# One woven sequence for the gate/up and down parts of each SwiGLU, in an order written out by hand, and weight splits in halves

## The chip, the cores and the metric

The kernel runs on one core of a Trainium2 chip. The metric is the device time of one execution in microseconds (us). A core has five engines that run side by side: TensorE (PE in the profile, with its weight loads as PEld), VectorE (DVE), ScalarE (ACT), GpSimd (POOL) and SyncE (SP), whose queue here issues the transfers. Each engine takes its instructions in the order in which the program lists them for it. SBUF is the on-chip memory; PSUM holds the results of matmuls in banks of 128x512 f32.

## What is computed

One layer over 1024 tokens of width 1024, all in f32. The change touches the two SwiGLUs (`D_FF` = 2816), and slightly the mixers and the cross-attention in between:

```python
def swiglu(h, w_gu, w_down):
    gu = h @ w_gu
    gate, up = jnp.split(gu, 2, axis=-1)
    return (jax.nn.silu(gate) * up) @ w_down

def reference(x, mem, ...):
    ...
        x = x + 0.5 * swiglu(rmsnorm(x, ffn1_norm[l]), ffn1_w_gu[l], ffn1_w_down[l])
        h = rmsnorm(x, mix_norm[l])
        proj = h @ w_in[l]
        ...
        x = x + mixed @ w_out[l]
        x = x + memory_cross_attention(rmsnorm(x, mem_q_norm[l]), rmsnorm(mem, mem_kv_norm[l]),
                                       mem_w_q[l], mem_w_kv[l], mem_w_o[l])
        x = x + 0.5 * swiglu(rmsnorm(x, ffn2_norm[l]), ffn2_w_gu[l], ffn2_w_down[l])
    return rmsnorm(x, final_norm)
```

## The kernel before

**Numbers in two parts.** Every f32 operand of a matmul is split into a rounded half `hi` (a Copy on ACT) and the remainder `lo` (a subtraction on DVE). A product is then three matmuls: hi by hi, hi by lo, lo by hi (`mm3`, L113 to L117).

**Layout.** x is held transposed in sixteen tiles `xT[c, hf]` of 128x512: `c` counts 128 columns of the model, `hf` the two halves of the tokens. `rs[hf]` holds 1/rms of each token, spread over the partitions; the lifted tiles `hT` (names hh and hl) hold x times the gain of the norm, and `rs` is multiplied in after the matmul.

**Seven products for eight.** `swiglu` (L547) cuts each pair of column blocks into a 2x2 of blocks and multiplies them by Strassen's scheme in Winograd's form. `PRODUCTS` (L212) lists the seven products of one job: the factor of the weights (A11, A12, A22 or a sum S1 to S4, made on POOL at L235 to L244), the factor of the activations (B11, B21, B22 or a sum T1 to T4), and the bank X, Y or Z into which the product is accumulated. A bank is read between products, since X passes from A11 to S2 to S3 to A22. A product of four blocks is twelve matmuls (L258 to L260).

**Jobs and weaving.** A `job` (L216) is the seven products of one pair of weight blocks: `factor` loads the weights on SP (L335), makes the sum on POOL, hi on ACT (L342) and lo on DVE (L343). `weave` (L263) takes two streams of jobs, the second three products behind the first (`LAG`), and alternates their products; `prepare` makes factors up to six products ahead (`AHEAD`). After each product `read` takes the bank: for gate/up an ACT copy (L615) or a DVE add (L622), then SiLU and two multiplications by `rs` (L632, L598, L599, L643); for down a DVE `scalar_tensor_tensor` into `xT` (L754).

**The order of a SwiGLU.** Eleven pairs of gate and up blocks come first. Pair 0 is multiplied plainly (gate before the call, up at L593 to L698). `sums` (L556) makes T1 to T4 from x, x is stored to DRAM and its tiles are given up (L677, L678) for tiles E of the gate/up results. Then `pairs.run()` (L708) weaves ten gate jobs with ten up jobs; each pair's result and its four sums are stored to DRAM (`store`, L683). Only after it comes a second weave (L763): down in groups of 4, 4 and 3 pairs (4, 4 and 2 in SwiGLU 2, with the last pair done plainly at its end), the pieces read back by `staged` (L715) through four buffers sg, the tiles of x by `fetch` (L725). In SwiGLU 1 the chunks of x that are finished are squared for the next norm and lifted for the mixers (`arrive`, L157; `lift_chunk`, L168). `normalise_memory` (L488) prepares the memory input beside pair 5 and later.

**What sets the order.** The program names operations in the order of the Python text, but the scheduler beneath places each engine's instructions by its own model of time and by when their operands are ready. An operation can so be put ahead of one that was written earlier. `tc.issue_after` fixes that one comes behind another on the same engine.

**Mixers and attention** load weights by columns (`load_cols`, L99, 128x8x128) or rows (`load_rows`, L108) and split them by `split` (L91): one ACT copy (L95) and one DVE subtraction (L96) of 1024 elements a partition.

Of the kernel before, what the change touches and what calls it, by code (L numbers as in the profile page):

```python
# [18 lines left out]
P = 128  # L19
# [12 lines left out]
def hybrid_layer(ctx, tc, x, mem, ffn1_norm, ffn1_w_gu, ffn1_w_down, mix_norm, w_in, hg_lb_raw,  # L32
# [37 lines left out]


# [19 lines left out]
    def split(pl, tag, src, shape=None, eng=None, bufs=None, ends="hl"):  # L91

        shape = shape or [P, src.shape[-1]]
        hi, lo = (pl.tile(shape, F32R, name=tag + end, bufs=bufs) for end in ends)
        nc.scalar.activation(hi, src, AF.Copy)  # L95
        (eng or nc.vector).tensor_tensor(lo, src, hi.bitcast(F32), op=ALU.subtract)  # L96
        return hi, lo
# [42 lines left out]
    def rsqrt(ss, n, scale, keep=""):  # L140
# [5 lines left out]
        nc.vector.tensor_scalar(ms, ss, scale, EPS, op0=ALU.mult, op1=ALU.add)  # L146
        nc.vector.tensor_scalar(b, ms.bitcast(I32), 1, None, op0=ALU.logical_shift_right)
        nc.vector.tensor_scalar(y.bitcast(I32), b, -1.0, RSQRT_SEED, op0=ALU.mult, op1=ALU.add)
        for _ in range(3):
            nc.vector.tensor_tensor(u, y, y, op=ALU.mult)  # L150
            nc.vector.scalar_tensor_tensor(u, u, -0.5, ms, op0=ALU.mult, op1=ALU.mult)
            nc.vector.scalar_tensor_tensor(y, u, 1.5, y, op0=ALU.add, op1=ALU.mult)
# [4 lines left out]
    def arrive(c, hf, g0, sqp, acc, lift=True, eng=None):  # L157

        sq = (accp if hf else sqp).tile([P, H], F32, name="sqa") if hf not in acc else sqp.tile([P, H], F32, name="sq", bufs=2)
        nc.scalar.activation(sq, xT[c, hf], AF.Square)  # L160
        if hf in acc:
            nc.gpsimd.tensor_tensor(acc[hf], acc[hf], sq, op=ALU.add)
        else:
            acc[hf] = sq
        if lift:
            lift_chunk(c, hf, g0, eng)

    def lift_chunk(c, hf, g0, eng=None):  # L168
        g = G[:, g0 + c:g0 + c + 1]
        hi = hp.tile([P, H], F32R, name=f"hh{c}_{hf}")  # L170
        lo = hp.tile([P, H], F32R, name=f"hl{c}_{hf}")
        nc.scalar.activation(hi, xT[c, hf], AF.Copy, scale=g)
        (eng or nc.vector).scalar_tensor_tensor(lo, xT[c, hf], g, hi.bitcast(F32), op0=ALU.mult, op1=ALU.subtract)
        hT[hf][c] = (hi, lo)

    def inv_rms(hf, acc, psn, tag):

        ps = psn.tile([P, H], F32, name=tag)
        for t in range(4):
            nc.tensor.matmul(ps[:, t:t + 1], acc[hf][:, t * P:(t + 1) * P], ones, start=True, stop=True)  # L180
        return rsqrt(ps[:, 0:4], 4, 1.0 / D, f"h{hf}")

    def inv_rms_both(acc, psn, tag):
        ps = psn.tile([P, H], F32, name=tag)
        for hf in range(2):
            for t in range(4):
# [1302 lines left out]
```

## Time and profile before

| | |
|---|---|
| time, median of 3 runs | 2348.41 us (2341.6, 2348.91, 2348.41) |
| the profiled execution | 2342.71 us |
| its span, first to last instruction | 2340.7 us |
| mean granted clock of TensorE in it | 0.987 |
| moved by DMA | 226.98 MB, mean 97 GB/s |

The profiled execution is one run; its span is 2.0 us less than its time. In the profile a row of the timeline gives the start, the duration, the engine, the line of the kernel, the operation, its output and inputs with their shapes, and in brackets how long the engine was idle before it and what it waited for. A group's row ends in the busy time and the mean of one in ns, then the idle time before and its causes. A waits row gives the total, how many times, and the longest. SwiGLU 1 fills the span from about 41 to 692 us, the mixers and the attention the time to about 1670, SwiGLU 2 the rest.

### The profile page before, as it was taken

To read this page: it belongs to the slowest core of one execution; us is meant where nothing else is said; L and a number is where in the kernel's file an instruction comes from. 1 tells how busy PE (TensorE), PEld (TensorE's weight loads), DVE (VectorE), ACT (ScalarE), POOL (GpSimd) and SP (SyncE) were. 2 spreads that over 40 slices of the span, in tenths; PEclk is the share of its full clock that TensorE was granted. 3 is DMA by queue.
4 is the path that set the end of the run, shared out by engine and by line. 5 is a ranking of instruction groups with operands and counts; after the bars stand their busy time and mean duration, and the time that the engine had idled before them with its cause. 6 is when DMAs were issued, how large, how long until landed. Compare 5 with 4: busy or idle time off the path is not lost.

```text
span 2340.7 us, 31188 instructions
## 1 busy us (share of the span) xinstructions
PE 2232.2 (95%) x11314; PEld 1869.8 (80%) x11314; DVE 1602.7 (68%) x2768; ACT 980.3 (42%) x1791; POOL 765.0 (33%) x720
## 2 busy tenths in 40 slices
PE   8899999889999999999999999999979999989998
PEld 6788878777878788887978888887768888877787
DVE  6755665768774878878697546567755555586777
ACT  6433443435454635345364333234533333343444
POOL 3555555522240202011022020001356565642223
PEclk9999999999999999999999999999989999999999
DMA  6232343465331000000014411111333333255432
GB/s 221 89 110 95 130 135 110 144 215 178 120 121 38 28 28 28 28 28 28 19 46 147 124 37 54 46 37 46 124 99 110 114 103 117 91 175 191 143 104 81
DMA packets 197529, 226.98 MB, mean 97 GB/s; under 512 B 10688, under 2 KB 139776, under 8 KB 197376
## 3 DMA queue, kind: packets, MB, share of 16 engines
q1 hardware_dynamic: 197376, 225.00, 29.7%
q8 instruction: 89, 1.46, 0.3%
q14 instruction: 64, 0.52, 0.1%
HBM read 165.45 MB, written 59.51 MB: 96 GB/s over the span
## 4 chain that ended last, share of the span: by engine, by line
PE 75%; DVE 12%; ACT 4%; issue 4%; POOL 3%; DMA 2%; SPq 0%; ACTq 0%; DVEq 0%; POOLq 0%
PE X L258 8%; PE X L259 8%; PE X L260 8%; PE acc L115 4%; PE acc L117 4%; PE acc L116 4%; PE Y L258 4%; PE Y L259 4%; PE Y L260 4%; DVE om L925 2%; PE Z L260 2%; PE Z L259 2%; PE Z L258 2%; PE q L115 2%; PE q L116 2%
## 5 line engine op out<-in xcount | busy, mean ns | idle before, releaser
L343 DVE TENSOR_TENSOR f<-S,f 128x512 fp32r<-128x512 f32 (+2 forms) x256 | 211.9, 830 | 175.6 <-ACT f L342 162.5
L342 ACT ACTIVATE f<-S 128x512 fp32r<-128x512 f32 (+2 forms) x256 | 155.1, 608 | 217.4 <-PE X L260 90.7
L258 PE MATMUL X<-T,f 128*128 128x512 f32 x488 | 196.3, 402 | 38.9 <-ACT E L615 15.4
L343 DVE TENSOR_TENSOR f<-r,f 128x512 fp32r<-128x512 f32 (+2 forms) x208 | 172.7, 833 | 65.8 <-ACT f L342 65.6
L258 PE MATMUL X<-hh,f 128*128 128x512 f32 x488 | 191.4, 392 | 14.2 <-DVE x L754 6.6
L259 PE MATMUL X<-T,f 128*128 128x512 f32 x488 | 195.0, 399 | 0.0
L260 PE MATMUL X<-T,f 128*128 128x512 f32 x488 | 194.8, 399 | 0.0
L342 ACT ACTIVATE f<-r 128x512 fp32r<-128x512 f32 (+2 forms) x208 | 125.6, 610 | 159.1 <-PE X L260 90.1
L259 PE MATMUL X<-hl,f 128*128 128x512 f32 x488 | 190.1, 389 | 0.0
L260 PE MATMUL X<-hh,f 128*128 128x512 f32 x488 | 190.0, 389 | 0.0
L235 POOL TENSOR_TENSOR S<-r,r 128x512 f32<-128x512 f32 (+2 forms) x64 | 95.2, 1488 | 188.3 <-DMA r<-in_ffn_w_down_dram 117.5
L115 PE MATMUL acc<-hh,wh 128*128 128x512 f32 (+1 forms) x384 | 152.8, 398 | 0.0
L117 PE MATMUL acc<-hh,wl 128*128 128x512 f32 (+1 forms) x384 | 145.2, 378 | 0.0
L116 PE MATMUL acc<-hl,wh 128*128 128x512 f32 (+1 forms) x384 | 144.6, 377 | 0.0
L258 PEld LDWEIGHTS X<-T,f 128*128 128x128 f32 x488 | 94.9, 195 | 61.7 <-ACT E L615 16.3
L922 POOL TENSOR_SCALAR_AFFINE_SELECT om<-om 128x128 f32<-128x128 f32 x64 | 25.4, 397 | 354.0 <-ACT om L917 353.8
L241 POOL TENSOR_TENSOR S<-r,S 128x512 f32<-128x512 f32 (+2 forms) x64 | 81.6, 1275 | 165.2 <-DVE f L343 162.2
L244 POOL TENSOR_TENSOR S<-r 128x512 f32<-128x512 f32 (+2 forms) x64 | 97.3, 1520 | 107.9 <-DVE f L343 99.3
L599 POOL TENSOR_TENSOR E<-E,rs 128x512 f32<-128x512 f32 x84 | 121.1, 1443 | 31.0 <-ACT E L598 25.8
L598 ACT ACTIVATE E<-E 128x512 f32<-128x512 f32 x84 | 52.9, 631 | 186.0 <-POOL E L632 165.8
L632 POOL TENSOR_TENSOR E<-E,rs 128x512 f32<-128x512 f32 x60 | 100.6, 1677 | 89.6 <-DVE E L622 89.6
L258 PEld LDWEIGHTS X<-hh,f 128*128 128x128 f32 x488 | 91.7, 188 | 37.2 <-ACT f L342 8.2
(451 smaller groups left out, 6449.9 us busy)
## 6 DMA issues: line engine op xcount, KB each, us to landing
r<-in_ffn_w_gu_dram SPq DMA_DIRECT2D x86, 512.0 KB
r<-in_ffn_w_down_dram SPq DMA_DIRECT2D x34, 512.0 KB
wraw<-in_w_in_dram SPq DMA_DIRECT2D x20, 512.0 KB
wraw<-in_mem_w_kv_dram SPq DMA_DIRECT2D x16, 512.0 KB
T<-in_x_dram SPq DMA_DIRECT2D x8, 512.0 KB
fx<-x SPq DMA_DIRECT2D x16, 256.0 KB
x<-fx SPq DMA_DIRECT2D x16, 256.0 KB
xs<-x SPq DMA_DIRECT2D x16, 256.0 KB
```

The costliest lines, as they stand in the source:

```text
L115: nc.tensor.matmul(ps, lh, rh, start=start, stop=False)
L116: nc.tensor.matmul(ps, lh, rl, start=False, stop=False)
L117: last_mm[0] = nc.tensor.matmul(ps, ll, rh, start=False, stop=stop).ins
L235: nc.gpsimd.tensor_tensor(src, a[1, 0], a[1, 1], op=ALU.add)
L244: nc.gpsimd.tensor_tensor(src, a[0, 0], a[1, 0], op=ALU.subtract)
L258: nc.tensor.matmul(ps, fh[:, i, :], bh, start=a, stop=False, skip_group_check=True)
L259: nc.tensor.matmul(ps, fh[:, i, :], bl, start=False, stop=False, skip_group_check=True)
L260: nc.tensor.matmul(ps, fl[:, i, :], bh, start=False, stop=z, skip_group_check=True)
L342: nc.scalar.activation(hi, src, AF.Copy)
L343: nc.vector.tensor_tensor(lo, src, hi.bitcast(F32), op=ALU.subtract)
L599: nc.gpsimd.tensor_tensor(s, s, rs[hf], op=ALU.mult)
L632: eng.tensor_tensor(out, src, rs[hf], op=ALU.mult)
```

## The change

1. A small class `in_order` wraps four engines. Whatever is issued through `dve`, `act`, `pl_` or `pe` is tied behind the operation last issued through it. Nearly everything in the SwiGLUs' streams uses these; the plain products, the splits of the mixers and other parts do not.

```diff
+    class in_order:
...
+        def __getattr__(self, name):
+            def issue(*args, **kw):
+                if self.last is None:
+                    done = getattr(self.eng, name)(*args, **kw)
+                else:
+                    with tc.issue_after(self.last):
+                        done = getattr(self.eng, name)(*args, **kw)
+                self.last = done.ins
+                return done
...
+    dve, act, pl_, pe = (in_order(eng) for eng in (nc.vector, nc.scalar, nc.gpsimd, nc.tensor))
```

2. A factor is made in four stages, each a fixed number of products ahead of its use; the pieces for down have leads of their own. `defer` runs a step so many products later.

```diff
-    AHEAD, LAG = 6, 3
+    LAG = 3
+    LOAD, SUM, FETCH, HI, LO, FETCHED_HI, FETCHED_LO = 7, 6, 7, 5, 4, 4, 3
...
+        def prepare(self, i, limit=None):
...
+            for stage in (4, 3, 2, 1):
+                for lead in (LO, LO - 1, HI, SUM, LOAD):
+                    if 0 <= i + lead < len(order):
+                        j, n = order[i + lead]
+                        if j.stages(n)[stage - 1][0] == lead and (limit is None or stage < 3 or i + lead < limit):
+                            j.upto(n, stage)
+            for what, lead in ((2, FETCHED_LO), (1, FETCHED_HI), (0, FETCH)):
+                if 0 <= i + lead < len(order):
+                    j, n = order[i + lead]
+                    if j.fetch:
+                        j.fetch(PRODUCTS[n][1], what)
```

3. The two weaves become one: the down jobs follow the gate and the up jobs in their streams.

```diff
+            streams = [[gate_job(p) for p in range(1, FP)], [up_job(p) for p in range(1, FP)]]
+            for p0, pn in GROUPS[:2] + last_group:
+                get, fetch = fetches(p0, pn)
+                for e in range(4):
+                    streams[e % 2].append(down_job(p0, pn, e, get, fetch))
+            pairs = weave(*streams)
```

4. Pieces land in the tile of their lo part, without the buffers sg, and are split there. Group 1's first reads copy on ACT into tiles E, the others add on DVE. The second multiplication by `rs` is left out for pairs under `NORMED` = 8, and done once for the sum of groups 1 and 2, in `to_x`, which also loads x.

```diff
+            def staged(p, bk, n):
+                hi, lo = slot(blk, bk, n)
+                nc.sync.dma_start(out=lo.bitcast(F32), in_=ad[p][bk])
+                return hi, lo
...
+            def to_x(c, hf):
...
+                t = pools["sg"].tile([P, H], F32, name="sg")
+                nc.sync.dma_start(out=t, in_=xd[c, hf])
+                pl_.tensor_tensor(xt, xt, rs[hf], op=ALU.mult)
+                pairs.defer(2, lambda: dve.scalar_tensor_tensor(xt, xt, 0.5, t, op0=ALU.mult, op1=ALU.add))
```

5. The start is taken apart. `flow` takes a step of each of several chains in turn: T1 and T2 (`sums_12`), the scaling and SiLU of pair 0 (`scaled`), the first factors; T4's half; then T4's rest, T3 and the stores of x during the first products.

```diff
+            flow([sums_12(j, pools["e0"].tile([P, H], F32, name="e") if j < 2 else tp.tile([P, H], F32, name="t"))
+                  for j in range(2)] + [between()]
+                 + [sums_12(j, tp.tile([P, H], F32, name="t")) for j in range(2, 4)], 3)
+            flow([sums_4(0), sums_4(1)], 2)
+            for m in range(2):
+                dve.tensor_tensor(s[0][m], s[0][m], ups[0][m], op=ALU.mult)
+            for m in range(2):
+                ups[1] = plain(up, m, 1, u_banks[2 + m])
+                dve.tensor_tensor(s[1][m], s[1][m], ups[1], op=ALU.mult)
+            pairs.start(to=2)
...
+            pairs.defer(1, lambda: flow([sums_4(2), sums_4(3)], 2))
+            pairs.defer(2, x_away)
+            pairs.defer(4, open_mp)
+            pairs.defer(14, lambda: store(0, s[0][0], s[1][0], s[0][1], s[1][1]))
+            pairs.run()
```

6. `normalise_memory` runs in smaller steps from pair 2 on, its rows loaded twice. In SwiGLU 1 finished chunks are lifted into slots that are free (`waiting`, `FREED`), and the squares of two chunks are added by matmuls and not on POOL (`apart`). In SwiGLU 2 the last pair's pieces and rows are fetched and split while group 3 runs.

7. `split` works in two halves where it splits weights loaded by columns:

```diff
-        nc.scalar.activation(hi, src, AF.Copy)
-        (eng or nc.vector).tensor_tensor(lo, src, hi.bitcast(F32), op=ALU.subtract)
+        n = shape[1]
+        for part in (slice(0, n // 2), slice(n // 2, n)) if tag == "w" and len(shape) == 3 else (slice(0, n),):
+            nc.scalar.activation(hi[:, part], src[:, part], AF.Copy)
+            (eng or nc.vector).tensor_tensor(lo[:, part], src[:, part], hi[:, part].bitcast(F32), op=ALU.subtract)
```

More of the change, by code (lines that the diff above doesn't have):

```diff
@@ L178, in inv_rms @@
         ps = psn.tile([P, H], F32, name=tag)
-        for t in range(4):
-            nc.tensor.matmul(ps[:, t:t + 1], acc[hf][:, t * P:(t + 1) * P], ones, start=True, stop=True)
+        sums_of_squares(ps, 0, acc[hf])
         return rsqrt(ps[:, 0:4], 4, 1.0 / D, f"h{hf}")
@@ L185, in inv_rms_both @@
         for hf in range(2):
-            for t in range(4):
-                nc.tensor.matmul(ps[:, 4 * hf + t:4 * hf + t + 1], acc[hf][:, t * P:(t + 1) * P], ones, start=True, stop=True)
+            sums_of_squares(ps, 4 * hf, acc[hf])
         y = rsqrt(ps[:, 0:8], 8, 1.0 / D, "h")
@@ L667, in swiglu @@
[L667 to L674 removed]
+                    dve.tensor_tensor(out, src, g[p][key], op=ALU.mult)
+                    if side and p >= 2:
+                        if "side" not in stack:
+                            stack["side"] = side(psx, "aux", pools["mp"])
+                        next(stack["side"], None)
@@ L763, in swiglu @@
[L763 to L771 removed]
+                xp.close()
```

533 lines of the change are left out of this document (325 added, 208 removed).

## The prediction

> **What bounds the kernel now.** I read the page's first two parts, then the span cut into stretches, then the waits of TensorE (PE), then the timeline around the long ones.
>
> ```profile
> span 2340.7 us, 31188 instructions
> PE 2232.2 (95%) x11314; PEld 1869.8 (80%) x11314; DVE 1602.7 (68%) x2768; ACT 980.3 (42%) x1791; POOL 765.0 (33%) x720
> ```
>
> PE is busy for 95% of the span and no instruction of its mathematics goes, so only two things can be won: its idle 108.5 us (2340.7 - 2232.2) and what it loses while its clock is low. The stretches show where both lie (columns: length, busy time of PE, PEld, DVE, ACT, POOL, granted clock, DMA share, GB/s).
>
> ```profile
> core 0: us, PE busy (x) PEld busy (x) DVE busy (x) ACT busy (x) POOL busy (x), PEclk, DMA share, GB/s
> ...
> 68.00:108.00 40.00, 33.92 (x135) 26.82 (x134) 30.28 (x46) 16.88 (x34) 24.73 (x17) 0.91 0.30 99
> 108.00:456.00 348.00, 345.26 (x1527) 284.75 (x1528) 216.83 (x302) 136.25 (x244) 194.24 (x133) 1.00 0.36 118
> 456.00:500.00 44.00, 31.90 (x123) 24.82 (x122) 34.75 (x49) 18.70 (x34) 17.05 (x10) 0.88 0.84 284
> 500.00:692.00 192.00, 188.35 (x830) 155.41 (x829) 142.49 (x207) 86.95 (x145) 62.37 (x49) 1.00 0.43 136
> 692.00:716.00 24.00, 16.70 (x76) 13.60 (x75) 15.15 (x28) 9.11 (x15) 6.77 (x8) 0.86 0.17 56
> 716.00:1700.00 984.00, 952.19 (x5644) 816.02 (x5643) 696.37 (x1442) 415.68 (x802) 142.91 (x238) 1.00 0.17 52
> 1700.00:1720.00 20.00, 7.97 (x26) 6.09 (x25) 11.11 (x16) 6.06 (x11) 11.07 (x8) 0.66 0.40 132
> 1720.00:2080.00 360.00, 359.97 (x1589) 297.73 (x1587) 214.29 (x277) 135.15 (x235) 208.96 (x143) 1.00 0.34 110
> 2080.00:2116.00 36.00, 25.56 (x92) 20.20 (x93) 28.12 (x37) 15.18 (x27) 11.95 (x8) 0.81 0.74 239
> 2116.00:2264.00 148.00, 145.65 (x642) 119.98 (x640) 106.14 (x156) 61.16 (x104) 39.33 (x32) 1.00 0.43 139
> 2264.00:2341.00 77.00, 67.61 (x372) 58.57 (x372) 57.72 (x132) 34.33 (x68) 25.61 (x28) 0.94 0.23 82
> ```
>
> I call the length less PE's busy time multiplied by its clock the loss of a stretch. In order: 9.1 us (40 - 33.92 x 0.91) where SwiGLU 1 starts its products, 2.7 in its gate/up, 15.9 where gate/up hands over to down, 3.7 in down, 9.6 where the mixers begin, 31.8 over mixers and attention, 14.7 at SwiGLU 2's start, 0 in its gate/up, 15.3 at its hand-over, 2.4 in down, 13.4 in the final tail. The change rewrites all of these but the mixers' middle and the tail: **73.4 us** are within its reach. In dense stretches a matmul takes 0.226 us (345.26/1527), so a product of twelve takes 2.71 us.
>
> What ended the idle time:
>
> ```profile
> 79.45 0.79 PE L258 MATMUL X<-T,f 128*128 128x512 f32 x1 [3.40 <-ACT E L615]
> 78.19 0.60 ACT L498 ACTIVATE aux<-mt 128x512 f32<-128x512 f32 x1 [3.74 <-DMA mt<-in_mem_dram]
> 470.63 0.80 PE L258 MATMUL X<-T,f 128*128 128x512 f32 x1 [6.45 <-DVE E L622]
> 466.41 0.68 DVE L622 TENSOR_TENSOR E<-Z,E 128x512 f32<-128x512 f32 x1
> 482.72 4.01 SPq L729 DMA_DIRECT2D x<-fx  x8
> 491.45 0.57 PE L258 MATMUL X<-T,f 128*128 128x512 f32 x1 [3.68 <-DVE x L754]
> 689.48 6.85 DVE L173 SCALAR_TENSOR_TENSOR hl<-x,G,hh 128x512 fp32r<-128x512 f32 x8
> 697.08 0.77 PE L258 MATMUL X<-T,f 128*128 128x512 f32 x1 [4.22 <-DVE x L754]
> 1697.09 5.25 POOL L244 TENSOR_TENSOR S<-r 128x512 f32<-128x512 f32 x1 [4.42 <-DVE T L578]
> 1711.44 0.63 ACT L342 ACTIVATE f<-S 128x512 fp32r<-128x512 f32 x1 [5.66 <-POOL S L238]
> 1712.61 0.80 PE L258 MATMUL X<-T,f 128*128 128x512 f32 x1 [12.03 <-ACT E L615]
> 2093.48 0.80 PE L258 MATMUL X<-T,f 128*128 128x512 f32 x1 [6.44 <-DVE E L622]
> ```
>
> The reader is to see one pattern: PE waits for a read of a bank that needs 0.6 to 0.7 us but stands in its engine's queue behind work nobody needs yet. At 78 us ACT waits for a row of the memory input ahead of the copy that frees X. At 466 the adds of the last gate/up products alternate with splits of the down factors. At 482 loads of x, eight in this row, go ahead of down's weights. At 689 DVE runs eight lifts for the mixers in a row while a read of X waits. At 1697 DVE's run of sums starves POOL (5.25 us), then ACT, and PE stands for 12 us.
>
> **The change part by part.**
>
> *Joining the phases.* Down jobs enter the same woven order, so no phase ends with the lone products of one stream, where a bank is needed again one product after its read. Bank X is now written again four positions later: three products, 8.1 us, of cover. The down factors' slots are free seven positions before their first use, which is the fetch lead, so the fetch has 7 x 2.71 = 19 us, with the split due 3 to 4 products ahead. Loads of x leave the hand-over; group 2's 16 `to_x` steps fetch them. This removes the causes at 466 and 482, and at 2080 to 2116. Late next is DVE itself, where a group's pieces are split:
>
> ```profile
> L754 DVE SCALAR_TENSOR_TENSOR x<-X,x 128x512 f32<-128x512 f32 x43 | 29.4, 687 | 25.8 <-PE X L260 25.7
> L720 DVE TENSOR_TENSOR hl<-sg,hh 128x512 fp32r<-128x512 f32 x28 | 22.7, 843 | 1.1 <-ACT hh L719 1.1
> L343 DVE TENSOR_TENSOR f<-S,f 128x384 fp32r<-128x384 f32 x16 | 10.2, 638 | 0.0
> L162 POOL TENSOR_TENSOR sqa<-sqa,sq 128x512 f32<-128x512 f32 x10 | 13.1, 1313 | 14.6 <-ACT sq L160 14.6
> ```
>
> Across a boundary of four-block groups, 14 positions (37.9 us) carry about 14 factor splits, 28 piece splits and 16 reads or sums: 58 x 0.69 = 40 us on DVE, 2 over; at the 0.843 of L720 for the pieces, 6 over, within the 8.1 us cover. I charge 2 us for each such boundary (bounds 0 and 8). Into group 3 of SwiGLU 1 (products of 2.03 us; 30.5 us) stand 14 x 0.64 + 21 x 0.69 + 14 x 0.69 + 8 x 0.69 for group 2's last `to_x` = 38.6 us, 8 over against 6.1 of cover: 2. In SwiGLU 2 group 3 has two blocks (1.36 us a product) and the last 12 pieces and 4 row factors are split in it too: some 4. The down parts with their hand-overs therefore keep 6 and 8 us, from 19.6 (15.9 + 3.7) and 17.7 (15.3 + 2.4): **25.3 us** gained.
>
> Group 1's copies move 16 reads to ACT and `to_x` returns 16 to DVE: nothing net. POOL gains 16 `to_x` products and loses the second multiplication by rs for eight pairs, 32, so 16 fewer.
>
> *The order by hand.* The memory rows now start with pair 2 in small steps, each load a step ahead of its use: ACT's 3.74 us goes. The sums start with T1 and T2; T3 and T4 follow during the first products. But `scaled` is DVE's first ordered instruction and needs rs, so all ordered DVE work queues behind it:
>
> ```profile
> 51.40 0.58 ACT L198 ACTIVATE rs<-nm 128x512 f32<-128x512 f32 x1
> 69.84 0.50 PE L258 MATMUL X<-hh,f 128*128 128x512 f32 x1 [1.43 <-DVE E L662]
> 1676.09 0.58 ACT L198 ACTIVATE rs<-nm 128x512 f32<-128x512 f32 x1
> 1692.71 0.39 PE L258 MATMUL X<-hh,f 128*128 128x512 f32 x1
> ```
>
> The woven products began at 69.8 and 1692.7 us, 17 and 16 us after rs was there. Up to T2's last split DVE has 16 operations of 0.7 us, 11, and some 3 us of turns with ACT: ready in time. Then come 13 (T4's half, SiLU products, first factors), 4 more sums and 8 for T3: 41 x 0.7 + 3 = 32 us after rs, while T3 is due at position five, 16.5 + 13.6 = 30. I keep 3 us at start 1 and 4 at start 2 (bounds: 0, and the present 9.1 and 14.7): **16.8 us** gained. The 2.7 us in gate/up I leave as they are: DVE, ACT and POOL are busy 62, 39 and 56% there.
>
> *The mixers' start.* Four lifts go to unused slots during e = 2 and twelve share the last eleven products (22 us of PE) with reads and splits: 12 x 0.69 + 11 x (0.64 + 0.69) = 23 us. The block of eight lifts disappears, and two squares skip POOL's 1.3 us add. I keep 3 of 9.6 us: **6.6** gained (bounds 0 and 9.6).
>
> *Splits in halves.*
>
> ```profile
> L96 DVE TENSOR_TENSOR wl<-wraw,wh 128x1024 fp32r<-128x1024 f32 x65 | 79.4, 1222 | 12.2 <-ACT wh L95 11.9
> L95 ACT ACTIVATE wh<-wraw 128x1024 fp32r<-128x1024 f32 x65 | 68.6, 1059 | 90.7 <-PE acc L116 41.8 <-PE wo L116 22.6 <-PE q L116 9.9
> L95 ACT ACTIVATE fh<-q 128x512 fp32r<-128x512 f32 x32 | 19.1, 596 | 72.5 <-PE q L117 49.0 <-DVE q L1341 23.5
> PE tr L944 <- DVE sq L827: 6.9, 4, 1.7
> ```
>
> Sixty column loads (68 splits of wraw in the program less the eight of w_o's rows) split twice at 0.60 and 0.69 us add 60 x 0.14 = 8 us of ACT and 60 x 0.16 = 9.5 of DVE, beside PE, with both engines 42 and 71% busy there. Against it, a chain operation waits behind 0.69 instead of 1.22 us, of the kind that held the transposes of L944 for 6.9 us. I take zero; without cover it costs 9.5, and the most it can win is that 6.9.
>
> **Sum.** 25.3 + 16.8 + 6.6 = 48.7 us. The profiled run took 2342.7 us (span plus 2.0), 5.7 below the median of 2348.4. 2342.7 - 48.7 = 2294; allowing some of that spread between a run and the median, I say **2297 us**.
>
> **The rivals.** (B) *DVE keeps up at the boundaries.* For it: from 500 to 692 us the same splits and reads run today and PE loses 3.7. Then the 14 us kept in the down parts go: 2283.
>
> (C) *DVE and POOL hold each other up.* For it: L720 takes 0.843 us at the mean beside 0.69 for a read of a bank, and L244 once took 5.25. If POOL's operations count on DVE's time, a boundary adds 8 sums of 1.3 us and the later ones four `to_x` each: 10 us over a cover already used, at three boundaries of each SwiGLU, 60; the stretch from 500 to 692, where DVE and POOL together show 204.9 us of 192 and PE loses 3.7, bears out perhaps a third: 20 more, 2317. The Trainium skill, "SBUF — State Buffer", section "SBUF: two separate sides", calls the pair's shared port an exclusive lock that one operation holds to its end; by that rule in full, an estimate, the time would be 2357. The trace agrees with it only in part: 204.9 us in 192 can't be so if each waits out the other without showing as busy.
>
> (D) *Fixed order stalls the steady state; slower.* A factor of a late weight load now stands ahead of reads on ACT.
>
> ```profile
> POOL S L235 <- DMA r<-in_ffn_w_gu_dram: 64.9, 21, 18.3
> ```
>
> Today POOL waits 3.1 us on average for such loads, 18.3 at worst, with no cost to PE. In the fixed order the load can start only when the buffer's last factor is split, and POOL's sum then holds ACT's factor and the copy of X behind it. It decides once a load is later than 8.1 us beyond its lead; at 2 us for each of 44 jobs it costs 88: 2385. It breaks even at 1.1 us a job. Against it: two products (5.4 us) lie between issue and use and four more before PE needs the factor.
>
> (E) *The stalls only move.* The starts are set by rs and the hand-overs by DVE's total work, so the wait falls elsewhere and some 45 us return: 2342.
>
> **How the numbers follow.** Forecast 0.52, B 0.17, C 0.16, E 0.06, D 0.09. A difference under 0.3% (7 us) counts as none. Forecast, B and C are faster: 0.85; E the same: 0.06; D slower: 0.09. The range reaches below B for a gain in the mixers and above C for its own spread and the splits' 9.5: 2272 to 2328; it leaves out D, E and the ends.
>
> **What would show it.** The stretches at the hand-overs should show PE at 95% or more and clock 1.00, with no idle over 3 us before L258's successor; ACT's wait for the memory row and SP's run of x loads should be gone. The starts should keep a gap at position five that waits for T3. The mixers' first stretch should lose about 3 us. Wrong would be PE waits for reads of banks in the middle of gate/up (D), DVE above 95% at boundaries with PE below 90% (C), or mixers that lose more than 40 us.

## The result, and the profile after

| | us |
|---|---|
| before, median of 4 runs beside it | 2348.29 (2341.6 to 2348.91) |
| after, median of 4 runs | 2324.39 (2320.99 to 2326.18) |
| after by before | 0.9904 (95% interval 0.9892 to 0.9917) |
| the profiled execution of after: its span | 2319.3 (before 2340.7) |
| mean granted clock in it | 0.991 (before 0.987) |

The change gains 24 us, where 51 were forecast. The page of the changed kernel, parts one and two:

```profile
span 2319.3 us, 31224 instructions
PE 2236.2 (96%) x11330; PEld 1869.4 (81%) x11330; DVE 1692.2 (73%) x2832; ACT 980.0 (42%) x1885; POOL 731.5 (32%) x686
```

The lines to look at are DVE and POOL. POOL does 34 operations and 33.5 us less than before, yet DVE is busy for 90 us more (1602.7 before) with 64 more operations. Sixty of these are the weight splits cut in halves, a group that takes only 6 us more (84.8 us in 68 operations before, 91.1 in 128 now). So most of the 90 us must be operations that became longer: the factor splits f<-S, 256 of them both times, take 255.3 us where they took 211.9.

The stretches, cut a little earlier than before's because everything comes earlier (columns: length, busy time of PE, PEld, DVE, ACT, POOL, granted clock, DMA share, GB/s):

```profile
64.00:104.00 40.00, 34.06 (x143) 27.44 (x142) 34.14 (x42) 21.97 (x38) 17.93 (x12) 0.96 0.21 66
104.00:440.00 336.00, 336.00 (x1491) 278.16 (x1491) 231.74 (x310) 128.42 (x236) 153.86 (x104) 1.00 0.39 127
440.00:484.00 44.00, 39.58 (x163) 31.04 (x162) 42.45 (x52) 27.34 (x51) 18.16 (x12) 0.96 0.65 224
484.00:612.00 128.00, 126.42 (x556) 103.83 (x556) 101.47 (x128) 48.56 (x89) 60.32 (x40) 1.00 0.50 155
612.00:656.00 44.00, 38.45 (x150) 29.32 (x149) 43.43 (x56) 21.13 (x42) 22.42 (x16) 0.92 0.46 151
656.00:684.00 28.00, 28.00 (x126) 23.17 (x125) 26.69 (x35) 15.16 (x28) 17.49 (x14) 1.00 0.27 97
684.00:708.00 24.00, 21.09 (x97) 18.38 (x96) 13.76 (x30) 8.80 (x16) 1.61 (x5) 0.79 0.29 87
708.00:1680.00 972.00, 943.96 (x5600) 810.16 (x5599) 679.89 (x1477) 411.64 (x846) 134.19 (x235) 1.00 0.17 52
1680.00:1704.00 24.00, 17.64 (x67) 13.77 (x66) 22.05 (x31) 13.48 (x23) 5.42 (x4) 0.86 0.19 61
1704.00:2056.00 352.00, 352.00 (x1555) 291.45 (x1554) 237.48 (x272) 128.01 (x228) 168.77 (x115) 1.00 0.36 118
2056.00:2092.00 36.00, 32.75 (x142) 26.00 (x141) 35.90 (x43) 23.30 (x45) 16.05 (x10) 1.00 0.66 228
2092.00:2224.00 132.00, 130.45 (x575) 107.41 (x574) 105.65 (x133) 51.86 (x97) 61.38 (x40) 1.00 0.47 145
2224.00:2264.00 40.00, 33.45 (x136) 24.44 (x135) 39.27 (x64) 13.85 (x35) 17.18 (x16) 1.00 0.26 87
```

The loss (length less PE's busy time multiplied by its clock) of each, beside the forecast:

| stretch | before | forecast | after |
|---|---|---|---|
| start of SwiGLU 1's products | 9.1 | 3 | 7.3 |
| its gate/up | 2.7 | 2.7 | 0 |
| its hand-over and down (440 to 684) | 19.6 | 6 | 6.0 + 1.6 + 8.6 + 0 = 16.2 |
| the mixers' start | 9.6 | 3 | 7.3 |
| start of SwiGLU 2's products | 14.7 | 4 | 8.8 |
| its hand-over and down (2056 to 2264) | 17.7 | 8 | 3.2 + 1.6 + 6.5 = 11.3 |

The clock is given to two digits, so over the 972 us of mixers and attention a loss is uncertain by some 5 us. There the start times of single matmuls serve better: from the mixers' first matmul to the first s of the attention it took 718.8 us before (700.56 to 1419.34) and 722.5 after (684.81 to 1407.34). So of the 15.8 us that the mixers begin earlier, 3.7 are given back in them. The final norm's first matmul comes 21.6 us earlier (2312.18, now 2290.55).

What PE waited for most in the changed kernel (columns: total us, times, longest), over the whole span:

```profile
PE X L83 <- DVE E L83: 14.1, 10, 2.5
PE X L83 <- ACT e L83: 10.8, 2, 6.0
```

L83 is the helper that ties operations into the written order; nearly every ordered instruction has that line now, so the tiles' names must tell them apart. The 6.45 us waits at the hand-overs are gone. In their place stand many reads of X on DVE of up to 2.5 us, and two long waits for an ACT copy of X into a tile e, one at each start. The third long one, 2.9 us for an ACT square sg, is the mixers' start. These three places carry the shortfall, and the runs take them one by one.

### The profile page after: what moved, and what is told of

It reads as the page before. It is cut to its first block, busy times and chain, and to the rows that moved or that the text cites. A ratio compares the mean times of both kernels' runs of the same rounds, so it can differ in the third digit from the quotient of the medians.

```text
span 2319.3 us, 31224 instructions
## 1 busy us (share of the span) xinstructions
PE 2236.2 (96%) x11330; PEld 1869.4 (81%) x11330; DVE 1692.2 (73%) x2832; ACT 980.0 (42%) x1885; POOL 731.5 (32%) x686
## 5 line engine op out<-in xcount | busy, mean ns | idle before, releaser
L83 PE MATMUL X<-T,f 128*128 128x512 f32 x1464 | 348.0, 393 | 14.7 <-ACT e L83 10.8
L83 PEld LDWEIGHTS X<-T,f 128*128 128x128 f32 x1464 | 276.7, 190 | 75.2 <-ACT e L83 11.7
L83 PE MATMUL X<-hh,f 128*128 128x512 f32 x975 | 316.1, 394 | 15.6 <-DVE E L83 14.1
L83 ACT ACTIVATE f<-S 128x512 fp32r<-128x512 f32 (+2 forms) x256 | 154.4, 608 | 347.0 <-POOL S L83 346.6
L83 DVE TENSOR_TENSOR f<-S,f 128x512 fp32r<-128x512 f32 (+2 forms) x256 | 255.3, 1005 | 27.4 <-ACT f L83 25.9
L83 PEld LDWEIGHTS X<-hh,f 128*128 128x128 f32 x975 | 185.2, 190 | 59.6 <-ACT f L83 9.2
L83 POOL TENSOR_TENSOR E<-E,rs 128x512 f32<-128x512 f32 x112 | 180.0, 1608 | 121.5 <-DVE E L83 104.3
L83 DVE TENSOR_TENSOR f<-r,f 128x512 fp32r<-128x512 f32 (+2 forms) x192 | 200.8, 1063 | 0.3
L83 POOL TENSOR_TENSOR S<-r,r 128x512 f32<-128x512 f32 (+2 forms) x64 | 97.0, 1515 | 316.1 <-DVE E L83 93.6
L83 PE MATMUL X<-hl,f 128*128 128x512 f32 x488 | 192.4, 394 | 2.8 <-DVE hl L83 2.8
L83 PE MATMUL Y<-T,f 128*128 128x512 f32 x732 | 177.0, 390 | 0.2 <-DVE T L83 0.2
L83 PEld LDWEIGHTS Y<-T,f 128*128 128x128 f32 x732 | 137.2, 188 | 29.6 <-DVE T L83 1.1
L83 PE MATMUL Z<-hh,f 128*128 128x512 f32 x488 | 160.7, 389 | 0.0
L83 PE MATMUL Y<-hh,f 128*128 128x512 f32 x488 | 160.7, 389 | 0.0
L83 POOL TENSOR_TENSOR S<-S,r 128x512 f32<-128x512 f32 (+2 forms) x64 | 82.3, 1286 | 211.6 <-DVE f L83 211.6
L83 ACT ACTIVATE E<-X 128x512 f32<-128x512 f32 x102 | 60.5, 594 | 192.8 <-PE X L83 192.8
L83 DVE TENSOR_TENSOR E<-X,E 128x512 f32<-128x512 f32 x98 | 67.3, 686 | 84.3 <-PE X L83 84.1
L117 ACT ACTIVATE wh<-wraw 128x512 fp32r<-128x512 f32 (+1 forms) x128 | 79.0, 654 | 103.1 <-PE acc L138 41.6
```

Of the source, the lines that this page charges most:

```text
L83: done = getattr(self.eng, name)(*args, **kw)
L117: nc.scalar.activation(hi[:, part], src[:, part], AF.Copy)
```

## The experiments

All edits are to the changed kernel unless another is named. Below, "the changed kernel" is at 2324.39 us, and every run has its own ratio to the kernel before.

**1. Is it the joining?** The two weaves are kept apart again, everything else as changed.

```diff
-            pairs = weave(*streams)
+            pairs = weave(*(jobs[:FP - 1] for jobs in streams))
+            pairs.order += weave(*(jobs[FP - 1:] for jobs in streams)).order
```

> The changed kernel with its sequence cut again between gate/up and down: the ten gate and ten up jobs are woven by themselves, then the down jobs, all in the order written by hand. Nothing else differs. If the join is what won the time at the hand-overs, two ends with lone products of one stream come back: some 6 to 10 us in each SwiGLU, 2336 to 2344 us. Rival: the hand-overs are set by VectorE's total work around them, so cutting the sequence costs under 3 us in each: 2325 to 2330.

Measured: 2320.36 us, 0.9888 (0.9869 to 0.9907) of before, against 0.9904 (0.9892 to 0.9917) for the changed kernel: no difference that can be told, if any a gain, and below both ranges expected. Its losses from 440 to 684 are 5.0, 1.6, 7.0 and 0 us, 13.5 together and no more than with the joining. So the interleaving of the phases, which the prediction put first, isn't what shortened the hand-overs. The cut undoes no more than that: `prepare` still makes factors and pieces for the first down jobs ahead across it.

**2. Is it the order by hand?** The helper returns the plain operation, so that the scheduler places each engine's instructions.

```diff
-            def issue(*args, **kw):
...
-            return issue
+            return getattr(self.eng, name)
```

> The changed kernel without the ties between operations of one engine: the scheduler places them as before the change; the join, the leads and the later start of T3 and T4 stay. If the hand order wins time by itself, stalls like the 12 us at the second start return: 2335 to 2350 us. Rival: the ties are what keeps reads of banks behind piece splits at the hand-overs; without them the reads go ahead and the time falls to 2305 to 2318.

Measured: 2334.77 us, 0.9945 (0.9929 to 0.996), just under the range expected. The written order is worth 10 us. Without it, and with the phases joined, the stretches from 440 to 684 lose 9.1, 2.1, 15.5 and 0 us, more than the 19.6 of the kernel before.

**3. The halves.**

```diff
-        for part in (slice(0, n // 2), slice(n // 2, n)) if tag == "w" and len(shape) == 3 else (slice(0, n),):
+        for part in (slice(0, n),):
```

> The changed kernel with the weight splits of the mixers and the attention in one instruction again. By the forecast the halves are worth nothing: 2321 to 2328 us. Rival: the halves are what won the 2 to 3 us between the first attention scores and the second SwiGLU; then 2326 to 2331. Rival: their 9 us of VectorE cost time; then 2316 to 2321.

Measured: 2330.84 us, 0.9928 (0.9911 to 0.9945): some 6 us slower than with halves, in the range of the first rival. The halves as the only edit to the kernel before:

> The kernel before with the weight splits in halves as the only edit. Theory (a chain operation waits behind 0.69 instead of 1.22 us, which takes away the 3.3 us stall of so): 3 to 7 us faster than before, 2341 to 2345. Rival (the 6 us that the halves were worth in the changed kernel belong to its rearranged loads of msl, which were 4.6 us late there without halves): within 2 us of before, 2346 to 2350.

Measured: 2343.98 us, 0.9986 (0.9975 to 0.9996), 3.4 us faster, or 1 to 6. The longest wait that they touch, in a row of PE's timeline each: the kernel before, and then the kernel before with halves.

```profile
1233.87 0.39 PE L962 MATMUL so<-wl,v1l 128*128 128x256 f32 x1 [3.33 <-DVE wl L952]
```

```profile
1230.07 0.39 PE L964 MATMUL so<-wl,v1l 128*128 128x256 f32 x1 [2.11 <-DVE wl L954]
```

The matmul waits for the end of a row of DVE operations that begins with a weight split. The wait shrinks but doesn't go. The split takes 1.22 us in the first row and its half 0.68 in the second, and another operation of the row (hk<-hf) falls from 1.45 to 0.40, so the shorter split is only part of the 1.2 us. The changed kernel without halves shows this wait too (3.27 us), and a second one, for a load that comes 4.58 us late (1.36 in the changed kernel):

```profile
1243.31 0.58 PE L138 MATMUL acc<-hl,wh 128*128 128x256 f32 x1 [4.58 <-DMA hl<-msl]
```

So the halves win about 3 us by themselves. Whether the later load is due to the larger splits too isn't settled by one profile of each.

**4. The starts.** In the changed kernel DVE's first ordered instruction needs rs, and all ordered DVE work stands behind it. The edit moves the scaling behind the two later sums.

```diff
             flow([sums_12(j, pools["e0"].tile([P, H], F32, name="e") if j < 2 else tp.tile([P, H], F32, name="t"))
-                  for j in range(2)] + [between()]
-                 + [sums_12(j, tp.tile([P, H], F32, name="t")) for j in range(2, 4)], 3)
+                  for j in range(2)]
+                 + [sums_12(j, tp.tile([P, H], F32, name="t")) for j in range(2, 4)] + [between()], 3)
```

> The changed kernel with the scaling of pair 0 (the operations that need rs) and the first factors put behind the sums for T1 and T2 in the written order, instead of ahead and between. If rs at the head of VectorE's order makes the starts late, VectorE begins some 5 us earlier in each and the waits of the third product (4.8 and 6.0 us) shrink to under 2: 2312 to 2320 us. Rival: the third product waits because the copy that frees X has no tile until T4's half is done and stands behind four factors on ScalarE, whose place does not change: 2322 to 2328.

Measured: 2308.93 us (2306.8 to 2312.34), 0.9834 (0.9818 to 0.985), 3 us below the range expected. One moved entry wins 15.5 us over the changed kernel by the medians, and 12.5 by the spans of the profiled executions (2319.3 to 2306.8). First DVE's timeline in the changed kernel, then with the edit:

```profile
47.89 0.69 DVE L80 TENSOR_TENSOR sg<-X,rs 128x512 f32<-128x512 f32 x1 [5.51 <-ACT rs L231]
48.50 0.74 DVE L83 SCALAR_TENSOR_TENSOR T<-S,G,T 128x512 fp32r<-128x512 f32 x1
```

```profile
41.70 0.75 DVE L80 SCALAR_TENSOR_TENSOR T<-S,G,T 128x512 fp32r<-128x512 f32 x1
...
50.76 0.69 DVE L83 TENSOR_TENSOR sg<-X,rs 128x512 f32<-128x512 f32 x1 [0.18 <-ACT rs L231]
```

With rs at the head, DVE stands for 5.51 us and begins nothing of T1 and T2 before 48.5; with the scaling behind, its first sum starts at 41.7 and the wait for rs is 0.18. What the delay reached, in the changed kernel, first on ACT and then on PE:

```profile
70.89 1.29 ACT L83 ACTIVATE T<-e 128x512 fp32r<-128x512 f32 x2 [3.72 <-DVE e L83]
72.09 1.13 ACT L83 ACTIVATE f<-r 128x512 fp32r<-128x512 f32 x2
73.13 1.13 ACT L83 ACTIVATE f<-S 128x512 fp32r<-128x512 f32 x2
74.17 0.57 ACT L83 ACTIVATE e<-X 128x512 f32<-128x512 f32 x1
```

```profile
74.80 4.44 PE L83 MATMUL X<-T,f 128*128 128x512 f32 x12 [4.84 <-ACT e L83]
1691.14 5.16 PE L83 MATMUL X<-T,f 128*128 128x512 f32 x12 [6.00 <-ACT e L83]
```

The copy of X that frees the bank stands in ACT's written order behind T4's hi parts and four factors, and T4's wait 3.72 us for DVE. PE loses 4.84 us at the first start and 6.00 at the second, each followed by matmuls at a lower clock. With the edit both waits are gone (PE is busy for all 40.00 us from 64 to 104), and the two starts lose 0 and 1.5 us. Up to the mixers' start it is 6.1 us earlier (684.67, now 678.59), and from the first s to the final norm 7.3 us shorter (883.2, now 875.9 us).

**5. The down parts: is it DVE's turn with POOL?** At the hand-overs DVE is 96 to 100% busy. The first edit takes POOL out of the down parts. It leaves out part of the computation: the four weight sums of each down job (plain blocks are used in their place) and the multiplication by rs in `to_x`.

```diff
+            if self.fetch:
+                self.src[n] = a[{"A11": (0, 0), "S1": (1, 0), "S2": (0, 0), "A12": (0, 1), "S3": (1, 0),
+                                 "S4": (0, 1), "A22": (1, 1)}[key]]
+                return
...
-                pl_.tensor_tensor(xt, xt, rs[hf], op=ALU.mult)
```

> The changed kernel without GpSimd's work for the down jobs: the weight sums S1 to S4 of down and the multiplication by rs in to_x are left out (plain blocks stand for the sums), every other instruction stays. If GpSimd and VectorE hold each other up, VectorE's splits of down factors and of pieces fall from 0.9 to 1.2 us to 0.55 (three blocks) and 0.69, and the two hand-overs with their down parts lose under 8 us together instead of 27: 2300 to 2308 us. Rival: VectorE's own count of operations is what limits there; then the splits' mean stays above 0.85 and the time falls by under 6 us.

Measured: 2290.44 us in one run, 34 us less and 10 below the range expected. From 440 to 656 PE loses 0.3 us in place of 16.2. What PE waits for from 440 to 684 us in the changed kernel is DVE alone: for its reads of X, in the row here, and 5.1 us for the pieces that it splits (hl and T).

```profile
PE X L83 <- DVE E L83: 6.4, 4, 2.5
```

PE waits for no factor there, so it isn't that POOL's sums come late. But the run computes less, so the next edits do the same arithmetic on DVE. In the first only `to_x` moves (`pl_` becomes `dve` in its line); in the second the four sums as well, one product later than POOL made them.

```diff
-            return ((LOAD, self.load), (SUM, self.sum), (HI - early, self.hi), (LO - early, self.lo))
+            return ((LOAD, self.load), (HI if self.fetch else SUM, self.sum), (HI - early, self.hi), (LO - early, self.lo))
...
+            eng = dve if self.fetch else pl_
...
-                pl_.tensor_tensor(src, a[1, 0], a[1, 1], op=ALU.add)
+                eng.tensor_tensor(src, a[1, 0], a[1, 1], op=ALU.add)
```

> The 16 multiplications of x by rs in to_x are made by DVE instead of POOL, in the changed kernel; everything else stays. Theory (an operation of POOL lengthens DVE's operations between two SBUF tiles beside it, 0.69 to about 1.8 us): each of the 16 costs DVE 0.69 us itself and frees it of about 1 us at another operation, so 0 to 8 us faster than the changed kernel: 2316 to 2324. Rival (DVE's own work decides at the boundaries, POOL's doesn't matter): 16 x 0.69 = 11 us more on DVE in each SwiGLU, at places where it is 96 to 99% busy: 2328 to 2346.

> As the run before, and the four sums of each down job are made by DVE too, one product later than POOL made them. POOL then has nothing to do in the down parts, as where they were left out, but all results are computed; DVE has 48 x 0.65 = 31 us more in each SwiGLU besides the 11 of to_x. Theory (POOL's share of the port is the cost): DVE's splits of factors and pieces fall from means of 0.9 to 1.2 us to 0.69, which takes about 20 us from DVE in each SwiGLU at the very places, and S no longer waits for POOL: 8 to 20 us faster than the changed kernel, 2304 to 2316. Rival (leaving POOL out won its 34 us because less had to be computed): 42 us more on DVE in each SwiGLU, slower, 2330 to 2350.

Measured: 2327.56 us with `to_x` alone, 0.9916 (0.9902 to 0.9931), no difference from the changed kernel that can be told, and between its theory and its rival. With the sums too, 2316.57 us, 0.9872 (0.9857 to 0.9887): 7.8 us faster, at the edge of what the theory gave and 13 off the rival, though DVE now makes 48 more sums in each SwiGLU besides `to_x`. DVE's groups between 484 and 612 us say why; first the changed kernel, then with the sums on DVE (columns after the bar: busy us, mean ns).

```profile
L83 DVE TENSOR_TENSOR f<-S,f 128x512 fp32r<-128x512 f32 x26 | 24.8, 960 | 2.7 <-ACT f L83 2.7
L83 DVE TENSOR_TENSOR f<-r,f 128x512 fp32r<-128x512 f32 x19 | 21.9, 1163 | 0.0
L83 DVE TENSOR_TENSOR hl<-hl,hh 128x512 fp32r<-128x512 f32 x19 | 16.2, 911 | 0.0
L83 DVE TENSOR_TENSOR E<-X,E 128x512 f32<-128x512 f32 x17 | 11.6, 683 | 9.6 <-PE X L83 9.6
```

```profile
L83 DVE TENSOR_TENSOR f<-S,f 128x512 fp32r<-128x512 f32 x26 | 17.9, 688 | 6.6 <-ACT f L83 6.6
L83 DVE TENSOR_TENSOR f<-r,f 128x512 fp32r<-128x512 f32 x18 | 12.1, 684 | 0.0
L83 DVE TENSOR_TENSOR hl<-hl,hh 128x512 fp32r<-128x512 f32 x19 | 11.8, 683 | 0.0
L83 DVE TENSOR_TENSOR E<-X,E 128x512 f32<-128x512 f32 x17 | 11.7, 687 | 4.5 <-PE X L83 4.2
```

Splits between two SBUF tiles fall from 960, 1163 and 911 ns to 688, 684 and 683; the read that has one input in a PSUM bank is 683 and 687, untouched. The stretch itself is the plainest line of the study:

```profile
484.00:612.00 128.00, 126.28 (x555) 103.60 (x555) 103.78 (x168) 50.91 (x94) 0.00 (x0) 1.00 0.52 161
```

DVE does 168 operations in 103.78 us with POOL empty, where it did 128 in 101.47 beside 40 of POOL's. It took over all 40 and is busy for 2.3 us more. The other side is in the same trace of the same kernel: in gate/up, where POOL still works, the mean of f<-S stays at 1069 ns. One place shows how a single row of splits is held; DVE and POOL in the changed kernel, then DVE with the sums moved:

```profile
542.21 4.69 DVE L83 TENSOR_TENSOR hl<-hl,hh 128x512 fp32r<-128x512 f32 x4
...
543.12 1.53 POOL L83 TENSOR_TENSOR S<-r,r 128x512 f32<-128x512 f32 x1 [10.83 <-DVE hl L83]
544.61 1.75 POOL L83 TENSOR_TENSOR S<-r,S 128x512 f32<-128x512 f32 x1
```

```profile
541.43 2.49 DVE L83 TENSOR_TENSOR hl<-hl,hh 128x512 fp32r<-128x512 f32 x4
```

Four splits take 2.49 us, and 4.69 where two sums of POOL lie beside them. DVE's wait shows as busy time: the row has no idle time in it, and it ends at 546.90, 0.54 us after POOL's second sum (546.36).

The whole trace of the changed kernel says the same of every such split. Of its 88 splits hl<-hl,hh, 63 have no operation of POOL beside them or begin before it does, and take 676 to 689 ns. The other 25 begin while one runs. They take 1216 to 1786 ns, and each ends 544 to 552 ns after POOL's operation. So it is with the factor splits of 128x512: the 96 of f<-S and the 71 of f<-r that take over 0.9 us all begin while an operation of POOL runs, and end 544 to 555 ns after it.

The Trainium skill, "SBUF — State Buffer", section "SBUF: two separate sides", states that a DVE operation with two SBUF inputs and a POOL operation that reads SBUF exclude each other for the whole instruction. The trace agrees: the splits have two SBUF inputs and wait out POOL's operation to its end, and the reads of a bank aren't held. The total is smaller than one wait for each POOL operation, about 24 us on DVE in this stretch beside 60.32 us of POOL, since only a split that begins second is held, and only for the rest.

Moving the work wins little all the same, since the freed time is spent on the sums: of the 34 us of the run with less computed, only 8 come back when all is computed. At 612 to 656 us DVE is still busy for 43.61 of 44 us, and the stretch still loses 5.3. PE's waits change with it: from 440 to 684 us those for reads of X on DVE fall from 6.4 to 0.3 us, and those for factors on ACT, of which there were none, are 3.6. The sums now come a product later; whether an earlier place for them wins more wasn't run.

**6. The rows of four pieces.** In the changed kernel four pieces are split in one row, with reads of banks behind them. The edit splits two at a time, one product apart.

```diff
-            for what, lead in ((2, FETCHED_LO), (1, FETCHED_HI), (0, FETCH)):
+            for what, lead in ((3, FETCHED_LO - 1), (2, FETCHED_LO), (1, FETCHED_HI), (0, FETCH)):
...
-                        for hi, lo in Bg[bk]:
+                        for hi, lo in (Bg[bk], Bg[bk][:2], Bg[bk][2:])[what - 1]:
```

> The changed kernel with the splits of a group's pieces two per product (three and two products ahead) instead of four in a row every second product. If it is the row of four in fixed order that holds up the read of a bank behind it, the hand-overs and down parts lose 10 us less: 2311 to 2317 us. Rival: the work in the stretch is too much whatever its order; then within 3 us of 2324. Rival: the pieces are now late for their products; then 2327 to 2335.

Measured: 2329.46 us, 0.993 (0.9912 to 0.9948). It helps nothing and costs perhaps 5 us, in the range of the last rival, and PE's waits from 440 to 684 us show that rival's mechanism:

```profile
PE X L83 <- DVE hl L83: 4.2, 6, 1.3
...
PE X L83 <- DVE E L83: 0.2, 1, 0.2
```

The row of four did hold the reads: PE's wait for them falls from 6.4 to 0.2 us. But the pieces now come late, and the waits for them (hl and T, to all banks) rise from 5.1 to 11.7 us. The four stretches lose 14.9 us where they lost 16.2, so the wait has moved within DVE's work. Where the 5 us fall isn't shown.

**7. The mixers' start.** Three lifts stand on DVE ahead of the last reads (changed kernel; DVE, then PE):

```profile
682.01 3.56 DVE L83 SCALAR_TENSOR_TENSOR hl<-E,G,hh 128x512 fp32r<-128x512 f32 x3
685.50 0.68 DVE L83 SCALAR_TENSOR_TENSOR E<-Y,E 128x512 f32<-128x512 f32 x1
```

```profile
689.13 0.58 PE L208 MATMUL nm<-ones,sg 128*128 128x1 f32 x2 [2.91 <-ACT sg L183]
```

```diff
-                                pairs.defer(1, lambda lo=lo: next(lo, None))
+                                pairs.defer(1 if e == 2 else 4, lambda lo=lo: next(lo, None))
```

> In the changed kernel the second halves of the last lifts (DVE's hl from x) are deferred by four products instead of one, so that they stand behind the last reads of the down banks. Theory (three lifts, 3.56 us of DVE at 682.0, held the read of Y at 685.5 and that of X at 687.4, so the squares came late, PE idled 2.9 us at 689.1 and ran at half clock behind it): the idle time falls under 1.5 us, the granted clock from 684 to 708 rises from 0.79 to over 0.9, and the time falls by 2 to 5 us, 2319 to 2322. Rival (ACT's squares and copies set the end, or PE then waits for the lifts instead): within 2 us of the changed kernel, 2322 to 2326.

Measured: 2326.41 us (2322.12 to 2330.62), 0.9903 (0.9886 to 0.992): nothing gained. Two of PE's rows and one of DVE's with the edit:

```profile
688.61 0.38 PE L208 MATMUL nm<-ones,sg 128*128 128x1 f32 x2 [1.20 <-ACT sg L183]
692.43 6.71 DVE L83 SCALAR_TENSOR_TENSOR hl<-E,G,hh 128x512 fp32r<-128x512 f32 x10
709.48 0.80 PE L137 MATMUL acc<-hh,wh 128*128 128x512 f32 x1 [3.74 <-DVE sq L1065]
```

The mechanism was read rightly: the wait falls from 2.91 to 1.20 us, and the clock from 684 to 708 rises from 0.79 to 0.93. But the lifts are needed all the same. Ten of them now stand in a row of 6.71 us in front of the mixers' own DVE work, and PE waits 3.74 us behind it. From the first sum of squares to the first score z it is 36.0 us with the edit (685.86 to 721.87) and 35.1 without (684.67 to 719.76). The rival held: the wait has only moved. The profiled execution is the slowest of its four (2330.62 us), and most of what makes it long lies later, where the edit changes nothing: from the first z to the first s it takes 695.5 us, where the changed kernel took 687.6.

**8. The causes together.**

> DVE makes the down parts' sums and to_x, and at the start all four sums of T1 and T2 stand ahead of the scaling by rs. Theory: the two causes lie in different stretches, so their gains add: 2308.9 less the 8 to 20 us of the sums on DVE, 2289 to 2301, with losses of about 2 us at both starts together and under 15 in both down parts. Rival: the sums on DVE lose, and the sum of both lies above 2310.

Measured: 2302.81 us (2299.18 to 2304.99), 0.981 (0.9793 to 0.9826). The starts and the sums add nearly in full: 15.5 and 7.8 from 2324.4 are 2301.1. It lies 2 us above the range expected.

> As the run with rs moved and all of POOL's work in the down parts on DVE, but the 16 multiplications of to_x stay with POOL. From the two single runs (to_x on DVE cost 3 us, with the sums 8 won): 2302.8 less 3, 2297 to 2303. Rival (any operation of POOL beside the splits costs DVE more than its own 0.69): 2303 to 2310.

Measured: 2302.35 us (2300.86 to 2305.39), 0.9802 (0.9788 to 0.9817). As expected, and the same as the run before: once the sums are gone from POOL, it doesn't matter which engine multiplies in `to_x`. This is the best of the versions that compute everything, 47 us below the kernel before in its own comparison (2349.77) and 22 below the changed one.

> rs behind the first sums, the sums of the down jobs on DVE, the last lifts late, and gate/up and down woven apart again. If the causes add (15.4, about 11, 2 to 5 and 4 us below the changed kernel's 2324.4): 2289 to 2295. If they overlap (one wait hidden behind another): 2296 to 2305.

Measured: 2311.16 us (2307.45 to 2312.91), 0.9836 (0.9819 to 0.9853): worse than either range. The two edits added to the version before it, with `to_x` on POOL (2302.35 us), cost 9 us together, and 7.3 by the spans of the profiled executions (2301.7, now 2309.0). The marks in the timeline place them: the mixers' first matmul comes 1.5 us later (674.90, now 676.39), from there to the first z it takes 39.6 us (to 715.95) where it took 35.1, and from the first s to the end 903.7 us where it took 903.3. So by their place the late lifts cost about 4.5 us, at the mixers' start. The unjoining has at most the 1.5 us ahead of them and the 0.4 at the end, too little to tell from nothing in one profile of each, and neither edit was run alone in this setting.

## Why the prediction was right or wrong

**The bound and the places were right.** PE lost its time at the starts, at the hand-overs and at the mixers' start, and the change gains there. The steady gate/up loses nothing in the fixed order, so rival D is out (its 44 jobs are 40, since pair 0 isn't woven). The time lies in the range, but the gain is less than half of the forecast, 24 us of 51. What happened in the down parts is the mechanism of rival C, with its tell (DVE 96, 99 and 98% busy at 440, 612 and 2224 us, PE at 90, 87 and 84%), and its 2317 is nearer than 2297. That nearness is partly luck: C put 20 us on the boundaries alone, 13.5 went missing there, and the rest of the shortfall comes from places that C doesn't name. The ground on which C was held low, 204.9 us of busy time in 192, falls: the wait is in the busy time (experiment 5).

**The step that failed first is the sum at the boundaries**, "58 x 0.69 = 40 us on DVE, 2 over; at the 0.843 of L720 for the pieces, 6 over, within the 8.1 us cover". It was mis-sized: 0.69 us is what a split takes when no operation of POOL holds it. Beside POOL's work it took 0.91 to 1.16 us in the mean. DVE's groups in the changed kernel from 440 to 484 us:

```profile
L83 DVE TENSOR_TENSOR hl<-hl,hh 128x512 fp32r<-128x512 f32 x16 | 14.3, 954 | 0.0
L83 DVE TENSOR_TENSOR f<-S,f 128x512 fp32r<-128x512 f32 x8 | 8.0, 1005 | 1.7 <-ACT f L83 1.7
L83 DVE TENSOR_TENSOR f<-r,f 128x512 fp32r<-128x512 f32 x6 | 6.2, 1048 | 0.0
```

Against the 683, 688 and 684 ns of the same splits with POOL empty, these 30 operations are 16 x 0.271 + 8 x 0.317 + 6 x 0.364 = 9.1 us longer. They come on top of the 2 us already over (the 6 holds some of them), and the cover is 8.1. The down parts kept 16.2 and 11.3 us in place of 6 and 8: 13.5 short. The rows for it were there; the same splits in gate/up of the kernel before (104 to 440 us):

```profile
L343 DVE TENSOR_TENSOR f<-S,f 128x512 fp32r<-128x512 f32 x69 | 63.1, 915 | 77.2 <-ACT f L342 68.0 <-issue 5.8 <-POOL S L244 2.9
L343 DVE TENSOR_TENSOR f<-r,f 128x512 fp32r<-128x512 f32 x53 | 51.7, 975 | 24.0 <-ACT f L342 24.0
```

The prediction took the price of a read from a bank instead, which POOL doesn't touch, and 0.843 for the pieces alone. Besides, the gain was added up wrongly: 19.6 + 17.7 less 14 is 23.3, not 25.3.

**The starts: the cause was named, its reach was not.** That `scaled` at the head of DVE's order holds everything until rs was in the prediction, and experiment 4 shows it. The step that failed is "T3 is due at position five, 16.5 + 13.6 = 30". PE didn't wait at position five for T3 but at position three for X, since the copy of X stood on ACT behind T4's halves. Only PE's need for the factors was followed, and not the engines' own orders behind the first wait. The starts kept 7.3 and 8.8 us in place of 3 and 4: 9.1 short.

**The mixers' start** kept 7.3 us in place of 3, 4.3 short. "The block of eight lifts disappears" is true of the block; three lifts in a row were left in front of the last reads, 3.56 us with their waits where 3 x 0.69 had been counted. Of the 7.3 us, 2.9 are idle time of PE and 4.4 the lower clock behind it, for which the sum had no term. Experiment 7 shows that the lifts can't be put off by four products either. From the mixers' first matmul to the first z it even takes 35.0 us, where it took 30.4 before (700.56 to 730.93), so what the last products won here was given back at once.

Those three and the slip of 2 us make 28.9. Less the 2.7 us that gate/up gained, which weren't forecast, it is 26.2, and the forecast missed by 27.4.

**The joining** got the credit in the prediction, and experiment 1 takes it away as far as the interleaving goes. Which part removed the long waits at the hand-overs isn't settled: the order by hand is worth 10 us over the whole kernel (experiment 2), and the pieces' new leads and the loads of x out of the way weren't undone alone.

**The halves** were taken at zero between a cost of 9.5 and a gain of 6.9. They gain 3.4 us alone, but not at the wait that was named. PE's wait for the transposes is 6.9 us with halves as without; the one that shrinks is for wl, from 4.6 to 2.3 us in all.

## What to carry to other kernels

Price an elementwise operation by the row of its own kind in the place where it will run, with the same neighbours: the same split took 0.69 us beside an idle POOL and 0.91 to 1.16 beside a busy one, and DVE's busy share hides this, since the wait counts as busy. Where DVE is the engine that runs out, an operation on POOL isn't free for it: taking 40 of them back cost DVE 2.3 us here. Look for less work or for another engine. In an order written by hand, look at the first instruction of each engine that needs a late value, and follow what stands behind it on every engine; moving one entry was worth 15.5 us, two thirds of the whole change.

## What the runs showed of the hardware

An operation of DVE with one input in a PSUM bank keeps its 0.68 to 0.69 us beside a busy POOL, and one with both inputs in SBUF that begins while POOL's operation runs ends 0.54 to 0.55 us after that (all 25 such splits hl in the changed kernel). Between 484 and 612 us all 40 operations of POOL, 60.32 us of it, were worth 2.3 us of DVE's busy time.

The longer of two idle times of PE can cost less clock. Behind 2.91 us, at 689.13 in the changed kernel, the matmuls run at half clock at once, and until 699.10. With the sums on DVE, behind 3.19 us, they keep their pace for 1.8 us more and then run at half clock from 687.08 to 693.98:

```profile
685.25 0.38 PE L208 MATMUL nm<-ones,sg 128*128 128x1 f32 x2 [3.19 <-ACT sg L183]
...
687.08 0.57 PE L208 MATMUL nm<-ones,sg 128*128 128x1 f32 x2
```

The Trainium skill, "TensorE: Matmul & The Clock Gate", section "Part 1: The HAM clock gate", says that the clock is set by a window of about 3.4 us that runs freely and isn't tied to the kernel's work. The two traces agree with that: the drop isn't tied to the end of the gap, and it lasts 10.0 and 6.9 us, near three and two such windows. So a stall's price can't be read from its length alone.
